# RMSNorm and SiLU on one core: one normalizing row in four moves from VectorE to GpSimd

## The chip, the cores and the metric

The kernel runs on one core of a Trainium2 chip. The metric is the device time of one execution in microseconds (us), as the median of several runs. The engines that matter here are VectorE (DVE in the profile), ScalarE (ACT), GpSimd (POOL) and SyncE (SP, which only issues loads and waits for stores). TensorE is not used.

## The reference

The input is x, 16 x 1024 rows of 512 float32 numbers, with a gamma of 512 numbers and a small eps. Each row is divided by its root mean square, multiplied by gamma, and put through SiLU:

```python
def reference(x, gamma, eps):
    rms = np.sqrt(np.mean(x ** 2, axis=-1, keepdims=True) + eps)
    x_norm = x / rms * gamma
    return (x_norm * (1.0 / (1.0 + np.exp(-x_norm)))).astype(np.float32)
```

33.55 MB are read and as many written. Gamma is drawn as ones, but the kernel multiplies by it all the same.

## The kernel before

The 16,384 rows lie 128 to a partition. One buffer in SBUF, `xb`, holds 96 rows for each partition and is used as a ring: a row is loaded into it, normalized in place, put through SiLU in place, and stored from it. Loads are transfers of 4 rows for each partition (1 MB) twice, then of 8, then seven of 16 (4 MB); stores are two of 8, six of 16 and two of 8. SyncE issues the loads in order; those of the last 32 rows wait for the stores that free their place in the ring. ScalarE issues the stores.

The unit of compute is a chunk of four rows for each partition, `cn = 4`, so that there are K = 32 units. All engines walk over the units k in order, each with its own written order, and meet at counting semaphores:

- ScalarE, `square(k)`: squares row 3 of the unit with a running sum into `ms` (L169), and rows 0 to 2 into a PSUM buffer `sq`, one of two (L176). In its order the steps are square(k), a store that is due, `swish(k - 2)`.
- VectorE, `sums(k)`: one reduction of the three squared rows from PSUM into `ms` (L218). Its order is sums(k), then `norm(k - 1)`.
- GpSimd: for each k it adds eps to four sums, `aeps` (L151, which waits for the reduction by `s_sum`), and raises them to the power -1/2, `rstd` (L158, which waits for L151 by `s_eps`). It announces the result by `s_rstd`.
- VectorE, `norm(k)`: four instructions, one for each row, each a multiply by the row's rstd and by gamma in one pass over 128x512 elements (L229). The first waits for `s_rstd`, the last announces `s_norm`.
- ScalarE, `swish(k)`: one SiLU over the four rows (L188), which waits for `s_norm` and announces `s_swish` to the stores.

Gamma comes in by a small transfer issued from ScalarE into `gamma4`, which GpSimd clears first (L146); VectorE spreads it over the partitions into `gamma_sb` (L242) between the first two reductions and announces `s_gamma`.

Of the kernel before, what the change touches and what calls it, by code (L numbers as in the profile page):

```python
# [9 lines left out]
def kernel(  # L10
# [7 lines left out]
    nc = tc.nc  # L18
    P = nc.NUM_PARTITIONS
    AF = mybir.ActivationFunctionType  # L20
    ALU = mybir.AluOpType
# [3 lines left out]
    xf = x.flatten_outer_dims()  # L25
    of = out.flatten_outer_dims()
    R, D = xf.shape

    groups = [8, 8] + [16] * 7
    G = len(groups)
    assert sum(groups) * P == R, R
    begin = [sum(groups[:g]) for g in range(G)]
    ring = 96
    loads = [(0, 0, 4), (0, 4, 4), (1, 0, 8)] + [(g, 0, 16) for g in range(2, G)]
    stores = [(0, 0, 8), (1, 0, 8)] + [(g, 0, 16) for g in range(2, G - 1)]
    stores += [(G - 1, 0, 8), (G - 1, 8, 8)]
    early = 2
    cn = 4  # L40
    n_sq = 3


    chunks = []
    new = list(range(len(loads)))
    for g in range(G):
        for c in range(0, groups[g], cn):
            need_now = [
                i for i in new if loads[i][0] == g and loads[i][1] < c + cn
            ]  # L50
            new = [i for i in new if i not in need_now]
            chunks.append(((begin[g] + c) % ring, need_now))
    assert not new
    K = len(chunks)

    ends = [-(-(begin[g] + r + n) // cn) for g, r, n in stores]

    inv_d = 1.0 / float(D)
    eps_f = float(eps)
# [6 lines left out]
    def sbuf(name, shape, dt=fp32):  # L66
        return nc.alloc_sbuf_tensor(name, shape, dt).ap()

    xb = sbuf("xb", [P, ring, D])
    gamma4 = sbuf("gamma4", [P, D])  # L70
    gamma_sb = sbuf("gamma_sb", [P, D])
# [4 lines left out]
    rstd = sbuf("rstd", [P, K, cn])  # L76
    sq = [nc.alloc_psum_tensor(f"sq{i}", [P, 4, D], fp32).ap() for i in range(2)]

    ld = [nc.alloc_semaphore(f"ld{t}") for t in range(len(loads))]
    st = [nc.alloc_semaphore(f"st{t}") for t in range(len(stores))]  # L80
    scratch = nc.dram_tensor("scratch", [P, 16], fp32, kind="Internal").ap()
    blank = sbuf("blank", [P, 16])
    s_blank = nc.alloc_semaphore("s_blank")
# [4 lines left out]
    s_gamma = nc.alloc_semaphore("s_gamma")  # L88
# [3 lines left out]
    s_eps = nc.alloc_semaphore("s_eps")  # L92
    s_rstd = nc.alloc_semaphore("s_rstd")
    s_norm = nc.alloc_semaphore("s_norm")
    s_swish = nc.alloc_semaphore("s_swish")

    def need(ins, sem, value):
        return ins.wait_op(sem, value, "sem-ge")

    def dram(ap, piece):  # L100
        g, r, n = piece
        rows = ap[begin[g] * P : (begin[g] + groups[g]) * P]
        return rows.rearrange("(p n) d -> p n d", n=groups[g])[:, r : r + n, :]

    def buf(piece):
        g, r, n = piece
        at = (begin[g] + r) % ring
        assert at + n <= ring
        return xb[:, at : at + n, :]


    stored_by_sync = set()

    def load(i):
        g, r, n = loads[i]
        old = begin[g] + r - ring
        for u, (h, q, m) in enumerate(stores):
            if (
                begin[h] + q < old + n and old < begin[h] + q + m
                and u not in stored_by_sync  # L120
            ):
                nc.sync.wait_ge(st[u], 16)
                stored_by_sync.add(u)
        return nc.sync.dma_start(
            out=buf(loads[i]), in_=dram(xf, loads[i])
        ).then_inc(ld[i], 16)

    entry = nc.main_func.blocks[0].instructions
    here = nc.cur_bb.bb.instructions
    for t in range(early):  # L130
        ins = load(t).ins
        assert here[-1] is ins or here[-1].name == ins.name
        here.pop()
        at = next(
            i for i, other in enumerate(entry)
            if other.engine == mybir.EngineType.SP
            and isinstance(other, mybir.InstDrain)
        )
        entry.insert(at, ins)
    for t in range(early, len(loads)):  # L140
        load(t)
    nc.sync.wait_ge(s_scratch, 16)

# [5 lines left out]
    for k in range(K):  # L149
        need(  # L150
            nc.gpsimd.tensor_scalar(  # L151
                out=aeps[:, k, :], in0=ms[:, k, :], scalar1=eps_f, scalar2=None,
                op0=ALU.add,
            ),
            s_sum, k + 1,
        ).then_inc(s_eps, 1)
        need(
            nc.gpsimd.tensor_tensor(  # L158
                out=rstd[:, k, :], in0=aeps[:, k, :], in1=neg_half, op=ALU.pow
            ),  # L160
            s_eps, k + 1,
        ).then_inc(s_rstd, 1)


    def square(k):
        at, landing = chunks[k]
        for i in landing:
            nc.scalar.wait_ge(ld[i], 16)  # L168
        acc = nc.scalar.activation(  # L169
            out=junk[k % 2], in_=xb[:, at + n_sq, :], func=AF.Square,  # L170
            scale=inv_d**0.5, accum_out=ms[:, k, n_sq : n_sq + 1],
        )
        if k >= 2:
            need(acc, s_acc, k - 1)
        acc.then_inc(s_acc, 1)
        square = nc.scalar.activation(  # L176
            out=sq[k % 2][:, 0:n_sq, :], in_=xb[:, at : at + n_sq, :],
            func=AF.Square, scale=inv_d**0.5,
        )
        if k >= 2:  # L180
            need(square, s_sum, k - 1)
        square.then_inc(s_sq, 1)

    def swish(k):
        at, _ = chunks[k]
        rows = xb[:, at : at + cn, :]
        need(
            nc.scalar.activation(out=rows, in_=rows, func=AF.Silu), s_norm, k + 1  # L188
        ).then_inc(s_swish, 1)

    def store(t):
        need(
            nc.scalar.dma_start(out=dram(of, stores[t]), in_=buf(stores[t])),
            s_swish, ends[t],
        ).then_inc(st[t], 16)

    need(nc.scalar.dma_start(out=scratch, in_=blank), s_blank, 1).then_inc(
# [7 lines left out]
    stored = 0  # L205
    for k in range(K + 3):
        if k < K:
            square(k)
        while stored < len(stores) and ends[stored] <= k - 2:
            store(stored)  # L210
            stored += 1
        if 2 <= k < K + 2:
            swish(k - 2)
# [9 lines left out]
        ).then_inc(s_sum, 1)  # L223

    def norm(k):
        at, _ = chunks[k]
        for j in range(cn):
            row = xb[:, at + j, :]
            ins = nc.vector.scalar_tensor_tensor(  # L229
                out=row, in0=row, scalar=rstd[:, k, j : j + 1], in1=gamma_sb,  # L230
                op0=ALU.mult, op1=ALU.mult,
            )
            if j == 0:
                need(ins, s_rstd, k + 1)
        ins.then_inc(s_norm, 1)

    for k in range(K + 1):
        if k < K:
            sums(k)
        if k == 0:  # L240
            need(
                nc.vector.stream_shuffle(gamma_sb, gamma4, [0] * 32), s_gld, 16  # L242
            ).then_inc(s_gamma, 1)
        if k == 1:
            nc.vector.wait_ge(s_gamma, 1)
        if k >= 1:
            norm(k - 1)


    for t in range(len(stores)):  # L250
        if t not in stored_by_sync:
            nc.sync.wait_ge(st[t], 16)

# [34 lines left out]
```

## Time and profile before

| what | us |
|---|---|
| three runs | 160.24, 160.31, 160.80 (median 160.31) |
| the profiled execution, whole | 160.24 |
| its span in the profile | 158.9 |
| VectorE busy | 138.9 (87%) |
| ScalarE busy | 125.4 (79%) |
| GpSimd busy | 90.1 (57%) |

The span runs from the first to the last instruction of the profile; the rest of the profiled execution's time lies around it. A line of a group of instructions reads: source line, engine, operation, output and inputs with their shapes, count; then busy us in all, mean ns of one; then the idle time of the engine just before them, and what ended most of it. In a timeline a line is start us, duration us, engine, source line, operation, and in brackets the idle time before it. Neighbouring instructions of one line are merged there (x4). In a table of windows, each engine's busy us in a stretch is followed by the count of its instructions; the last three numbers are TensorE's granted clock (not used here), the busy share of the DMA engines, and GB/s moved.

### The profile page before, as it was taken

How to read it: one execution, taken by the hardware profiler on the slowest of the kernel's cores; microseconds unless marked ns; L12 is line 12 of the kernel's file. 1: busy time of each engine (PE TensorE's matmuls, PEld its weight loads, DVE VectorE, ACT ScalarE, POOL GpSimd, SP SyncE). 2: the span in 40 equal slices, each digit the busy share in tenths (PEclk: the TensorE clock that was granted, in tenths of full speed). 3: DMA queues.
4: the chain of work that ended last, by engine and by line, in shares of the span. 5: the costliest groups of instructions: out<-in, count | busy, mean ns of one | idle time of the engine just before them, and what ended most of it. 6: DMA issues, size and time to landing. Idle time of an engine off the chain costs nothing.

```text
span 158.9 us, 436 instructions
## 1 busy us (share of the span) xinstructions
DVE 138.9 (87%) x162; ACT 125.4 (79%) x129; POOL 90.1 (57%) x71
## 2 busy tenths in 40 slices
DVE  0149999999999999999999999999999999999300
ACT  0845988888888889988888888888998898883600
POOL 2035444444455555588888899888888874445000
DMA  7999999999999999999999999999999999999896
GB/s 239 439 481 429 396 462 392 400 433 421 429 447 404 433 429 489 404 404 478 429 398 421 487 412 412 478 421 404 412 495 412 412 454 437 412 412 495 359 450 280
DMA packets 3035, 67.15 MB, mean 423 GB/s; under 512 B 468, under 2 KB 468, under 8 KB 472
## 3 DMA queue, kind: packets, MB, share of 16 engines
q1 hardware_dynamic: 1440, 33.56, 49.9%
q10 hardware_dynamic: 1592, 33.57, 49.1%
q14 instruction: 3, 0.02, 0.0%
HBM read 33.56 MB, written 33.56 MB: 422 GB/s over the span
## 4 chain that ended last, share of the span: by engine, by line
DMA 54%; DVE 34%; ACT 4%; issue 1%; POOL 0%; ACTq 0%; POOLq 0%
DMA xb<-in_x_dram 31%; DVE xb L229 22%; DMA out_dram<-xb 18%; DVE ms L218 12%; DMA gamma<-in_gamma_dram 5%; ACT xb L188 2%; ACT sq L176 1%; ACT junk L169 0%; DVE gamma_sb L242 0%; POOL gamma L146 0%; POOL blank L145 0%; ACTq L168 0%; POOLq L64 0%
## 5 line engine op out<-in xcount | busy, mean ns | idle before, releaser
L229 DVE SCALAR_TENSOR_TENSOR xb<-xb,rstd,gamma_sb 128x512 f32<-128x512 f32 x128 | 88.1, 770 | 0.0
L151 POOL TENSOR_SCALAR aeps<-ms 128x4 f32<-128x4 f32 x32 | 50.5, 1577 | 50.9 <-DVE ms L218 50.9
L188 ACT ACTIVATE xb<-xb 128x2048 f32<-128x2048 f32 x32 | 61.2, 1911 | 17.4 <-DVE xb L229 17.4
L218 DVE TENSOR_REDUCE ms<-sq 128x3 f32<-128x1536 f32 x32 | 56.8, 1774 | 7.3 <-ACT sq L176 7.2
L176 ACT ACTIVATE sq<-xb 128x1536 f32<-128x1536 f32 x32 | 45.9, 1434 | 0.0
L158 POOL TENSOR_TENSOR rstd<-aeps,neg_half 128x4 f32<-128x4 f32 x32 | 38.8, 1212 | 2.7
L169 ACT ACTIVATE junk<-xb 128x512 bf16<-128x512 f32 x32 | 19.8, 618 | 3.9 <-DMA xb<-in_x_dram 3.9
L169 ACT ACTIVATION_READ_ACCUMULATOR junk<-xb 128x1 f32 x32 | 6.0, 188 | 0.0
L204 ACT ACT_TABLE_LOAD x1 | 1.3, 1283 | 3.6 <-issue 3.6
L242 DVE LOAD_MASK_SELECT gamma_sb<-gamma x1 | 0.0, 14 | 2.2 <-DMA gamma<-in_gamma_dram 2.2
L145 POOL MEMSET blank<- 128x16 f32 x1 | 0.1, 112 | 1.5 <-POOLq L64 1.5
L242 DVE STREAM_SHUFFLE gamma_sb<-gamma 128x512 f32<-128x512 f32 x1 | 0.7, 716 | 0.0
L146 POOL MEMSET gamma<- 128x512 f32 x1 | 0.5, 526 | 0.0
L269 POOL MEMSET const-float32-0.0<- 128x1 f32 x1 | 0.1, 99 | 0.2 <-issue 0.2
L269 POOL MEMSET const-uint8-127<- 128x1 uint8 x1 | 0.1, 103 | 0.0
L269 POOL MEMSET const-bfloat16-1.0<- 128x1 bf16 x1 | 0.1, 102 | 0.0
L147 POOL MEMSET neg_half<- 128x4 f32 x1 | 0.1, 102 | 0.0
L269 POOL MEMSET const-float32-1.0<- 128x1 f32 x1 | 0.1, 99 | 0.0
## 6 DMA issues: line engine op xcount, KB each, us to landing
xb<-in_x_dram SPq DMA_DIRECT2D x7, 4096.0 KB, 49.5
out_dram<-xb ACTq DMA_DIRECT2D x6, 4096.0 KB, 29.0
out_dram<-xb ACTq DMA_DIRECT2D x4, 2048.0 KB, 15.0
xb<-in_x_dram SPq DMA_DIRECT2D x2, 1024.0 KB, 6.1
xb<-in_x_dram SPq DMA_DIRECT2D x1, 2048.0 KB, 10.7
scratch<-blank ACTq DMA_DIRECT2D x1, 8.0 KB, 8.0
gamma<-in_gamma_dram ACTq DMA_DIRECT2D x1, 8.0 KB
```

Of the source, the lines that this page charges most:

```text
L145: nc.gpsimd.memset(blank, 0.0).then_inc(s_blank, 1)
L146: nc.gpsimd.memset(gamma4, 0.0).then_inc(s_zero, 1)
L151: nc.gpsimd.tensor_scalar(out=aeps[:, k, :], in0=ms[:, k, :], scalar1=eps_f, scalar2=None, op0=ALU.add,),
L158: nc.gpsimd.tensor_tensor(out=rstd[:, k, :], in0=aeps[:, k, :], in1=neg_half, op=ALU.pow),
L169: acc = nc.scalar.activation(out=junk[k % 2], in_=xb[:, at + n_sq, :], func=AF.Square, scale=inv_d**0.5, accum_out=ms[:, k, n_sq : n_sq + 1],)
L176: square = nc.scalar.activation(out=sq[k % 2][:, 0:n_sq, :], in_=xb[:, at : at + n_sq, :], func=AF.Square, scale=inv_d**0.5,)
L188: nc.scalar.activation(out=rows, in_=rows, func=AF.Silu), s_norm, k + 1
L204: nc.scalar.preload_act_table_set("silu_and_others")
L218: nc.vector.tensor_reduce(out=ms[:, k, 0:n_sq], in_=sq[k % 2][:, 0:n_sq, :], op=ALU.add, axis=mybir.AxisListType.X,),
L229: ins = nc.vector.scalar_tensor_tensor(out=row, in0=row, scalar=rstd[:, k, j : j + 1], in1=gamma_sb, op0=ALU.mult, op1=ALU.mult,)
L242: nc.vector.stream_shuffle(gamma_sb, gamma4, [0] * 32), s_gld, 16
L269: nc = _bacc.Bacc("TRN2", target_bir_lowering=False, num_devices=1)
```

## The change

VectorE's `norm` covers three rows of a unit (`n_vec = 3`). GpSimd normalizes the fourth with two instructions after each rstd: a multiply by the row's rstd, and a multiply by `gamma_sb`, both in place over 128x512 elements; the second waits for the first by the new semaphore `s_scaled`, and announces `s_rest`. Before its first such row GpSimd waits for `s_gamma`. ScalarE's `swish(k)` waits for `s_rest` besides `s_norm`. The lists of transfers are written in another way, with one size for loads and stores alike, so that the first two stores move 4 rows each in place of one of 8, and the last load of 16 rows becomes two of 8. The lines below leave out what only renames.

```diff
-    groups = [8, 8] + [16] * 7
+    sizes = [4, 4, 8] + [16] * 6 + [8, 8]
     ring = 96
-    loads = [(0, 0, 4), (0, 4, 4), (1, 0, 8)] + [(g, 0, 16) for g in range(2, G)]
-    stores = [(0, 0, 8), (1, 0, 8)] + [(g, 0, 16) for g in range(2, G - 1)]
-    stores += [(G - 1, 0, 8), (G - 1, 8, 8)]
     early = 2
     cn = 4
     n_sq = 3
+    n_vec = 3
...
+    s_rest = nc.alloc_semaphore("s_rest")
+    s_scaled = nc.alloc_semaphore("s_scaled")
...
             s_eps, k + 1,
         ).then_inc(s_rstd, 1)
+        if k == 0:
+            nc.gpsimd.wait_ge(s_gamma, 1)
+        _, at, _ = chunks[k]
+        for j in range(n_vec, cn):
+            row = xb[:, at + j, :]
+            done = k * (cn - n_vec) + j - n_vec
+            need(
+                nc.gpsimd.tensor_scalar(
+                    out=row, in0=row, scalar1=rstd[:, k, j : j + 1], scalar2=None,
+                    op0=ALU.mult,
+                ),
+                s_rstd, k + 1,
+            ).then_inc(s_scaled, 1)
+            ins = need(
+                nc.gpsimd.tensor_tensor(out=row, in0=row, in1=gamma_sb, op=ALU.mult),
+                s_scaled, done + 1,
+            )
+        ins.then_inc(s_rest, 1)
...
     def swish(k):
-        at, _ = chunks[k]
+        _, at, _ = chunks[k]
         rows = xb[:, at : at + cn, :]
+        nc.scalar.wait_ge(s_rest, k + 1)
         need(
             nc.scalar.activation(out=rows, in_=rows, func=AF.Silu), s_norm, k + 1
         ).then_inc(s_swish, 1)
...
     def norm(k):
-        at, _ = chunks[k]
-        for j in range(cn):
+        _, at, _ = chunks[k]
+        for j in range(n_vec):
             row = xb[:, at + j, :]
             ins = nc.vector.scalar_tensor_tensor(
                 out=row, in0=row, scalar=rstd[:, k, j : j + 1], in1=gamma_sb,
```

More of the change, by code (lines that the diff above doesn't have):

```diff
@@ L27 @@
     R, D = xf.shape
-    groups = [8, 8] + [16] * 7
-    G = len(groups)
-    assert sum(groups) * P == R, R
-    begin = [sum(groups[:g]) for g in range(G)]
+    sizes = [4, 4, 8] + [16] * 6 + [8, 8]
     ring = 96
-    loads = [(0, 0, 4), (0, 4, 4), (1, 0, 8)] + [(g, 0, 16) for g in range(2, G)]
-    stores = [(0, 0, 8), (1, 0, 8)] + [(g, 0, 16) for g in range(2, G - 1)]
-    stores += [(G - 1, 0, 8), (G - 1, 8, 8)]
     early = 2
@@ L41 @@
     n_sq = 3
[L44 to L53, printed above, removed]
-    K = len(chunks)
-    ends = [-(-(begin[g] + r + n) // cn) for g, r, n in stores]
+    n_vec = 3
+    N = sum(sizes)
+    assert N * P == R, (N, R)
+    tiles = []
+    done = 0
+    for sz in sizes:
+        assert done % ring + sz <= ring
+        tiles.append((done * P, sz, done % ring))
+        done += sz
+    T = len(tiles)
+    chunks = [
+        (t, r, r == at)
+        for t, (_, sz, at) in enumerate(tiles)
+        for r in range(at, at + sz, cn)
+    ]
+    K = len(chunks)
+    ends = []
+    e = 0
+    for sz in sizes:
+        e += sz // cn
+        ends.append(e)
     inv_d = 1.0 / float(D)
@@ L77 @@
     sq = [nc.alloc_psum_tensor(f"sq{i}", [P, 4, D], fp32).ap() for i in range(2)]
-    ld = [nc.alloc_semaphore(f"ld{t}") for t in range(len(loads))]
-    st = [nc.alloc_semaphore(f"st{t}") for t in range(len(stores))]
+    ld = [nc.alloc_semaphore(f"ld{t}") for t in range(T)]
+    st = [nc.alloc_semaphore(f"st{t}") for t in range(T)]
     scratch = nc.dram_tensor("scratch", [P, 16], fp32, kind="Internal").ap()
@@ L98, in need, with dram, buf, load @@
         return ins.wait_op(sem, value, "sem-ge")
[L100 to L109, printed above, removed]
-    stored_by_sync = set()
[L114 to L126, printed above, removed]
+    def dram(ap, t):
+        first, sz, _ = tiles[t]
+        return ap[first : first + P * sz].rearrange("(p n) d -> p n d", n=sz)
+    def buf(t):
+        _, sz, at = tiles[t]
+        return xb[:, at : at + sz, :]
+    stored_by_sync = set()
+    def load(t):
+        _, sz, at = tiles[t]
+        waits = [
+            u for u in range(t)
+            if tiles[u][2] < at + sz and at < tiles[u][2] + tiles[u][1]
+            and u not in stored_by_sync
+        ]
+        for u in waits:
+            nc.sync.wait_ge(st[u], 16)
+            stored_by_sync.add(u)
+        return nc.sync.dma_start(out=buf(t), in_=dram(xf, t)).then_inc(ld[t], 16)
     entry = nc.main_func.blocks[0].instructions
@@ L139 @@
         entry.insert(at, ins)
-    for t in range(early, len(loads)):
+    for t in range(early, T):
         load(t)
@@ L162 @@
         ).then_inc(s_rstd, 1)
+        if k == 0:
[16 more added lines that the diff above has]
+        ins.then_inc(s_rest, 1)
     def square(k):
-        at, landing = chunks[k]
-        for i in landing:
-            nc.scalar.wait_ge(ld[i], 16)
+        t, at, first = chunks[k]
+        if first:
+            nc.scalar.wait_ge(ld[t], 16)
         acc = nc.scalar.activation(
@@ L192, in store @@
         need(
-            nc.scalar.dma_start(out=dram(of, stores[t]), in_=buf(stores[t])),
-            s_swish, ends[t],
+            nc.scalar.dma_start(out=dram(of, t), in_=buf(t)), s_swish, ends[t]
         ).then_inc(st[t], 16)
@@ L208 @@
             square(k)
-        while stored < len(stores) and ends[stored] <= k - 2:
+        while stored < T and ends[stored] <= k - 2:
             store(stored)
@@ L247 @@
             norm(k - 1)
-    for t in range(len(stores)):
+    for t in range(T):
         if t not in stored_by_sync:
```

## The prediction, made before the changed kernel was run

> **What bounds the kernel now.** I read the page first: engine totals, DMA, chain, groups.
>
> ```profile
> span 158.9 us, 436 instructions
> DVE 138.9 (87%) x162; ACT 125.4 (79%) x129; POOL 90.1 (57%) x71
> DMA packets 3035, 67.15 MB, mean 423 GB/s; under 512 B 468, under 2 KB 468, under 8 KB 472
> DMA 54%; DVE 34%; ACT 4%; issue 1%; POOL 0%; ACTq 0%; POOLq 0%
> ...
> L229 DVE SCALAR_TENSOR_TENSOR xb<-xb,rstd,gamma_sb 128x512 f32<-128x512 f32 x128 | 88.1, 770 | 0.0
> L151 POOL TENSOR_SCALAR aeps<-ms 128x4 f32<-128x4 f32 x32 | 50.5, 1577 | 50.9 <-DVE ms L218 50.9
> ```
>
> VectorE looks like the one to relieve, but the chain is mostly DMA. The windows by stage say why:
>
> ```profile
> 11.00:46.00 35.00, 34.82 (x42) 29.14 (x31) 16.37 (x16) 1.00 1.01 429
> 46.00:126.00 80.00, 80.00 (x93) 71.44 (x73) 59.95 (x37) 1.00 1.00 431
> 126.00:150.00 24.00, 22.36 (x28) 19.02 (x18) 11.67 (x10) 1.00 1.00 433
> 150.00:159.00 9.00, 0.00 (x0) 0.37 (x1) 0.00 (x0) 1.00 0.84 360
> ```
>
> The last two numbers of a row are the DMA's busy share and GB/s: from 11 to 150 us the transfers are full at about 431 GB/s. VectorE is full too, so two limits lie on top of each other, and relieving VectorE alone frees nothing that the transfers can use.
>
> The odd row is L151: adding eps to 128x4 numbers averages 1,577 ns. GpSimd's timeline shows it:
>
> ```profile
> 1.95 0.53 POOL L146 MEMSET gamma<- 128x512 f32 x1
> 2.41 0.10 POOL L147 MEMSET neg_half<- 128x4 f32 x1
> 9.09 0.23 POOL L151 TENSOR_SCALAR aeps<-ms 128x4 f32<-128x4 f32 x1 [6.57 <-DVE ms L218]
> 9.40 1.04 POOL L158 TENSOR_TENSOR rstd<-aeps,neg_half 128x4 f32<-128x4 f32 x1
> 13.62 0.66 POOL L151 TENSOR_SCALAR aeps<-ms 128x4 f32<-128x4 f32 x1 [3.18 <-DVE ms L218]
> 14.36 1.39 POOL L158 TENSOR_TENSOR rstd<-aeps,neg_half 128x4 f32<-128x4 f32 x1
> ...
> 65.40 2.65 POOL L151 TENSOR_SCALAR aeps<-ms 128x4 f32<-128x4 f32 x1 [2.19 <-DVE ms L218]
> 68.13 1.04 POOL L158 TENSOR_TENSOR rstd<-aeps,neg_half 128x4 f32<-128x4 f32 x1
> ```
>
> and VectorE's beside it:
>
> ```profile
> 65.20 2.76 DVE L229 SCALAR_TENSOR_TENSOR xb<-xb,rstd,gamma_sb 128x512 f32<-128x512 f32 x4
> 67.85 1.78 DVE L218 TENSOR_REDUCE ms<-sq 128x3 f32<-128x1536 f32 x1
> ```
>
> At 9.09 VectorE is idle: 0.23 us. At 13.62 the four multiplies have just begun and the same add takes 0.66, ending as the first of them ends. At 65.40 it takes 2.65, ending when all four have ended. So a GpSimd instruction that reads SBUF gets nowhere while VectorE's two-input multiply runs; it slips in between two of them (16 of 32 units) or is locked out until all are over (15). The reduction, which reads PSUM, does not hold it: the power at 68.13 keeps its 1.04 beside it. Today all this is free, because VectorE asks for rstd one reduction later than it is ready.
>
> **The change, part by part.** *Off VectorE:* one multiply of four per unit. Their pitch is 0.66 us (67.85-65.20 over 4), the reduction's is 1.66; a unit goes from 4.32 to 3.65 us, 21 us over 32 units. Alone this is worth nothing, with the DMA at share 1.00 to 150 us.
>
> *Onto GpSimd:* a 128x512 multiply by rstd and a 128x512 multiply by gamma per unit. No such row exists. The memsets give the cost of 512 columns in one pass: 0.53-0.10 = 0.43 us. One input: 0.23 (the free add) + 0.43 = 0.66; bounds 0.53 (the memset itself) and 1.09 (read and write passes in turn). Two inputs: 0.23 + 2x0.43 = 1.09, the operands read in turn; bounds 0.66 (all passes together) and 1.52 (three in turn). I take 0.66 and 1.09, the middles, since the memset shows one pass and nothing shows a second stream.
>
> [...]
>
> *What queues behind them.* GpSimd runs in order: the add and power for unit k+1 now stand behind both multiplies of unit k, and VectorE's multiplies of k+1 wait for that power. GpSimd alone needs 0.66 + 1.09 + 0.23 + 1.04 = 3.02, with four waits of 0.08 (9.40 less the add's end at 9.32) 3.34 us per unit. That would fit. But VectorE's three multiplies are released by the same semaphore, s_rstd, as GpSimd's first, and the two exclude each other. Locked out: 0.08 + 1.99 (three pitches) + 0.11 (770 less 660 ns, the last one's end) + 0.66 + 0.08 + 1.09 + 0.08 + 0.23 + 0.08 + 1.04 = 5.44 us. Slipping in by turns, VectorE first: 0.08 + 0.66 + 0.66 + 0.66 + 1.09 + 0.66 + 0.23 + 0.08 + 1.04 = 5.16. By turns, GpSimd first, the third VectorE multiply falls beside the power: 0.08 + 0.66 + 0.66 + 1.09 + 0.66 + 0.66 + 1.04 = 4.85. The trace has slips and lockouts about evenly, so I take (5.44 + 5.00)/2 = 5.22 us per unit. Whether VectorE is held by a running GpSimd pass in turn isn't shown; if it isn't, GpSimd is held instead, and the sum stands.
>
> [...]
>
> *ScalarE* gets a second wait before each silu (for s_rest). Behind it stand the squares of the unit three later, two 5.22 us cycles before they are needed; silu, square and reduction take 1.91 + 2.25 + 1.76 = 5.9 of these 10.4, so it costs nothing. *Stores and loads:* the first store splits into two of 4 rows, the last load into two of 8; one more issue each (0.34 us on ScalarE's queue, which waits 17.4 us in all today), same bytes: nothing.
>
> **The sum**, on the profiled execution (160.24 us, span 158.9, so 1.3 around it; the median shown is 160.31):
> - Unit 0's passes start when gamma lands (11.9) and end at 13.9; VectorE's first three multiplies then run, and rstd of unit 1 is ready at 16.2 (slip) to 17.3 (lockout): 16.8.
> - 30 units at 5.22: 156.6, to 173.4.
> - The last unit's multiplies on both engines: 0.08 + 2.10 + 0.66 + 0.08 + 1.09 = 4.0, to 177.4.
> - Last silu 1.91 and its wait: 2.0, to 179.4.
> - Last store. Before, issue at 150.40 to the end took 8.5; 3.24 MB (360 GB/s in 9 us) moved after 150.0, 2.10 of them its own, 0.17 before the issue, so 0.97 MB, 2.2 us, belonged to the store ahead. At the slower pace that one is done: 6.3, to 185.7.
> - Around the span 1.3: **187.0 us**. In short 30.4 + 30c, c the cycle.
>
> **The rivals.** *The passes interleave* (not slower). If a 512-column pass of GpSimd isn't stopped by the multiplies, only a 4-column one waiting at its first read, then c is 3.34 for GpSimd and 3.65 for VectorE, both under the transfers; the time stays 160.2, a few tenths either way, for the DMA had share 1.00. It decides from c = 4.3 down (30.4 + 30x4.3 = 159.4). For it: VectorE itself never stretched when GpSimd slipped in (pitch 0.66 in both). Against: 2.65 for a four-column add; and at the bounds of cost below, by turns, c is only just 4.29. Chance 0.10, of which 0.03 faster.
>
> *Dear passes.* At 1.09 and 1.52 with lockout c is 6.30, and the last unit grows by 0.86: 220 us. For it: GpSimd's power takes 1.04 for four columns, so its arithmetic can be slow. Chance 0.11.
>
> *Always by turns* is the forecast's own low side: 30.4 + 30x5.0 = 180.4; always locked out 193.6.
>
> **How the numbers follow.** The forecast's case, exclusion at middling prices, holds 0.79. About half of the spread of the bounds either way of 5.22 gives c of 4.65 to 5.8: 169.9 to 204.4, so 170 to 205. What is left out is the two rivals, 0.21. Half a percent (0.8 us) is about what a measurement can tell here; faster 0.03, same 0.07, slower 0.90.
>
> **What would show it.** Right: VectorE gains an idle group before its first multiply, released by GpSimd's power, of 1 to 2 us per unit; GpSimd's idle before the eps add falls from 50.9 us to nearly none and its busy share passes 90%; the chain runs over GpSimd's lines; the DMA share falls to about 0.85. The step on the multiplies is right if each takes longer than 0.66 and 1.09 only where VectorE's multiplies lie beside it. Wrong: VectorE's wait stays at zero, or passes of 512 columns keep one duration whether VectorE multiplies or not (interleaving), or take over 1.1 and 1.5 with VectorE idle (dear).

## The result and the profile after

The changed kernel takes 177.63 us (four runs, 177.50 to 177.64), against 160.34 us for the kernel before (four runs, the three shown before among them): a ratio of 1.107, 95% interval 1.1048 to 1.1092. It is 17.3 us slower. The forecast was 187.0 us in a range of 170 to 205, with a chance of 0.90 for slower. The profiled execution took 177.64 us, its span 176.3. (Of two kernels below, seven of ten executions without the gamma pass and one of two with half-width passes took 5 to 8 us longer than the fastest of the same kernel, for a cause that isn't known; these enter no comparison of times.)

The page of the changed kernel, its totals, its chain and the groups of the steps at issue:

```profile
span 176.3 us, 504 instructions
DVE 155.5 (88%) x130; ACT 125.2 (71%) x129; POOL 149.0 (85%) x135
POOL 84%; DMA 5%; issue 4%; ACT 1%; DVE 0%; POOLq 0%; ACTq 0%
...
L246 DVE SCALAR_TENSOR_TENSOR xb<-xb,rstd,gamma_sb 128x512 f32<-128x512 f32 x96 | 103.8, 1133 | 1.2 <-POOL rstd L157 1.2
...
L169 POOL TENSOR_SCALAR xb<-xb,rstd 128x512 f32<-128x512 f32 x32 | 51.0, 1594 | 4.9 <-DVE gamma_sb L259 1.8
L176 POOL TENSOR_TENSOR xb<-xb,gamma_sb 128x512 f32<-128x512 f32 x32 | 43.7, 1365 | 2.7
...
L150 POOL TENSOR_SCALAR aeps<-ms 128x4 f32<-128x4 f32 x32 | 20.7, 648 | 6.4 <-DVE ms L235 6.4
```

The chain now runs over GpSimd for 84% of the span, and its 50.9 us of idle time before the eps add are down to 6.4. The first surprise is VectorE: it has a quarter fewer multiplies, yet is busy for longer, 155.5 against 138.9 us. Each multiply takes 1,133 ns in the mean where it took 770. Its wait for GpSimd is inside its instructions, and shows in no idle column.

The windows of the changed kernel, in the columns explained before:

```profile
11.00:46.00 35.00, 34.84 (x31) 25.68 (x28) 32.20 (x28) 1.00 1.01 427
46.00:126.00 80.00, 80.00 (x67) 63.86 (x68) 75.65 (x66) 1.00 1.01 429
126.00:164.00 38.00, 36.76 (x32) 27.98 (x28) 35.88 (x33) 1.00 0.70 297
```

To 126 us the transfers are still full, loading ahead into the ring; then the share falls to 0.70, because the remaining stores wait for compute. VectorE shows 80.00 of 80 us busy and GpSimd 75.65, the rest being semaphore waits of 0.07 to 0.09 us between its instructions: both look saturated at once. The timeline of one unit says how that can be (ScalarE's lines are left out):

```profile
85.81 1.58 POOL L169 TENSOR_SCALAR xb<-xb,rstd 128x512 f32<-128x512 f32 x1
86.08 3.28 DVE L246 SCALAR_TENSOR_TENSOR xb<-xb,rstd,gamma_sb 128x512 f32<-128x512 f32 x3
...
87.47 1.35 POOL L176 TENSOR_TENSOR xb<-xb,gamma_sb 128x512 f32<-128x512 f32 x1
88.80 0.66 POOL L150 TENSOR_SCALAR aeps<-ms 128x4 f32<-128x4 f32 x1
89.29 1.75 DVE L235 TENSOR_REDUCE ms<-sq 128x3 f32<-128x1536 f32 x1
...
89.54 1.04 POOL L157 TENSOR_TENSOR rstd<-aeps,neg_half 128x4 f32<-128x4 f32 x1
```

A unit takes 4.87 us (the next first pass starts at 90.68). Shorter windows of the same timeline show the three multiplies one by one. The second runs from 86.96 to 87.70; the first and the third are:

```profile
86.08 0.95 DVE L246 SCALAR_TENSOR_TENSOR xb<-xb,rstd,gamma_sb 128x512 f32<-128x512 f32 x1
...
87.62 1.75 DVE L246 SCALAR_TENSOR_TENSOR xb<-xb,rstd,gamma_sb 128x512 f32<-128x512 f32 x1
```

The third multiply starts 0.15 us after GpSimd's gamma pass and ends 0.55 us after that pass ends (88.82), where the shortest of the 96 multiplies takes 0.735: it stood until the pass was over, or nearly so. Then GpSimd's eps add, which takes 0.23 at 8.88 with VectorE idle, stands in turn until that multiply ends, and takes 0.66. The rstd pass is another matter: it runs 1.58 us, and VectorE's first multiply starts and ends inside it, only some 0.2 us longer than the usual 0.735. So in this order the rstd pass holds VectorE at most near its start, and the gamma pass holds it nearly throughout.

### The profile page after: what moved, and what is told of

The parts are those of the page before. It is cut to its first block, busy times and chain, and to the rows that moved or that the text cites. A ratio compares the mean times of both kernels' runs of the same rounds, so it can differ in the third digit from the quotient of the medians.

```text
span 176.3 us, 504 instructions
## 1 busy us (share of the span) xinstructions
DVE 155.5 (88%) x130; ACT 125.2 (71%) x129; POOL 149.0 (85%) x135
## 3 DMA queue, kind: packets, MB, share of 16 engines
q10 hardware_dynamic: 1736, 33.57, 44.8%
q1 hardware_dynamic: 1584, 33.56, 44.8%
## 4 chain that ended last, share of the span: by engine, by line
POOL 84%; DMA 5%; issue 4%; ACT 1%; DVE 0%; POOLq 0%; ACTq 0%
POOL xb L169 29%; POOL xb L176 25%; POOL rstd L157 19%; POOL aeps L150 11%; DMA gamma<-in_gamma_dram 5%; ACT xb L206 1%; DVE gamma_sb L259 0%; POOL gamma L145 0%; POOL blank L144 0%; ACTq L204 0%; POOLq L163 0%; POOLq L66 0%
## 5 line engine op out<-in xcount | busy, mean ns | idle before, releaser
L246 DVE SCALAR_TENSOR_TENSOR xb<-xb,rstd,gamma_sb 128x512 f32<-128x512 f32 x96 | 103.8, 1133 | 1.2 <-POOL rstd L157 1.2
L235 DVE TENSOR_REDUCE ms<-sq 128x3 f32<-128x1536 f32 x32 | 55.8, 1745 | 7.0 <-ACT sq L193 7.0
L169 POOL TENSOR_SCALAR xb<-xb,rstd 128x512 f32<-128x512 f32 x32 | 51.0, 1594 | 4.9 <-DVE gamma_sb L259 1.8
L176 POOL TENSOR_TENSOR xb<-xb,gamma_sb 128x512 f32<-128x512 f32 x32 | 43.7, 1365 | 2.7
L157 POOL TENSOR_TENSOR rstd<-aeps,neg_half 128x4 f32<-128x4 f32 x32 | 33.5, 1048 | 2.7
L150 POOL TENSOR_SCALAR aeps<-ms 128x4 f32<-128x4 f32 x32 | 20.7, 648 | 6.4 <-DVE ms L235 6.4
```

The source lines that it names most:

```text
L150: nc.gpsimd.tensor_scalar(out=aeps[:, k, :], in0=ms[:, k, :], scalar1=eps_f, scalar2=None, op0=ALU.add,),
L157: nc.gpsimd.tensor_tensor(out=rstd[:, k, :], in0=aeps[:, k, :], in1=neg_half, op=ALU.pow),
L169: nc.gpsimd.tensor_scalar(out=row, in0=row, scalar1=rstd[:, k, j : j + 1], scalar2=None, op0=ALU.mult,),
L176: nc.gpsimd.tensor_tensor(out=row, in0=row, in1=gamma_sb, op=ALU.mult),
L235: nc.vector.tensor_reduce(out=ms[:, k, 0:n_sq], in_=sq[k % 2][:, 0:n_sq, :], op=ALU.add, axis=mybir.AxisListType.X,),
L246: ins = nc.vector.scalar_tensor_tensor(out=row, in0=row, scalar=rstd[:, k, j : j + 1], in1=gamma_sb, op0=ALU.mult, op1=ALU.mult,)
```

## The experiments

**The lists alone.** VectorE takes all four rows again, and GpSimd no passes; the new lists of transfers stay. The edit takes out the passes and the wait of `swish` for `s_rest` as well.

```diff
-    n_vec = 3
+    n_vec = 4
...
```

> Only the new lists of loads and stores, with VectorE normalizing all four rows and GpSimd none. If the lists cost nothing (prediction): 160.3 us, within 0.3 either way, VectorE's unit at 4.32 us. Rival, the two small early stores or the split last load disturb the transfers: 161 us or more with a DMA share under 1.00 between 11 and 150 us.

Measured: 160.09 us, ratio 0.9976 (0.9965 to 0.9988). The lists cost nothing; they are even a quarter of a percent ahead of the kernel before. Where the 0.4 us come from isn't settled. So the whole loss, 17.5 us against this kernel, belongs to the moved row.

**VectorE out of the way.** Its multiplies shrink to 16 columns.

```diff
-                out=row, in0=row, scalar=rstd[:, k, j : j + 1], in1=gamma_sb,
-                op0=ALU.mult, op1=ALU.mult,
+                out=row[:, 0:16], in0=row[:, 0:16], scalar=rstd[:, k, j : j + 1],
+                in1=gamma_sb[:, 0:16], op0=ALU.mult, op1=ALU.mult,
```

> VectorE's three multiplies cover 16 of 512 columns (the other 496 of rows 0 to 2 stay unnormalized), so that VectorE hardly reads SBUF; GpSimd's work is whole. Theory A, GpSimd's own work fills its cycle: its passes stay at 1.58 and 1.35 us, only the eps add falls from 0.66 to 0.23, the cycle goes from 4.87 to about 4.44 and the time to 177.6 - 30 x 0.43 = 165 us. Theory B, exclusion as in the prediction: the passes fall to about 0.66 and 1.09, the cycle to 3.3, and the transfers bound the time at 160 us.

Measured: 162.70 us, ratio 1.0133 (1.0112 to 1.0153). Two lines of the timeline and the group of the add:

```profile
87.05 1.69 POOL L169 TENSOR_SCALAR xb<-xb,rstd 128x512 f32<-128x512 f32 x1
88.82 1.26 POOL L176 TENSOR_TENSOR xb<-xb,gamma_sb 128x512 f32<-128x512 f32 x1
```
```profile
L150 POOL TENSOR_SCALAR aeps<-ms 128x4 f32<-128x4 f32 x32 | 7.4, 231 | 6.4 <-DVE ms L235 6.4
```

The passes are dear by themselves: 1.69 and 1.26 us with only the narrow multiplies beside the first (1.58 in the first two units), far from the 0.66 and 1.09 of the forecast. But the cycle is 4.45 us (from 82.60 to 87.05), so with these prices alone GpSimd would lose 2 us, not 17. Theory A's cycle was right; its time, 165, was 2.3 us high, mostly since the start and the last unit also lose their collisions (rstd of unit 1 is ready at 16.2 instead of 17.4, and from the last rstd to the last silu it takes 3.2 instead of 3.7).

**No gamma pass.**

```diff
...
-            ins = need(
-                nc.gpsimd.tensor_tensor(out=row, in0=row, in1=gamma_sb, op=ALU.mult),
-                s_scaled, done + 1,
             )
```

> GpSimd's second pass, the multiply by gamma, is left out for the fourth row (gamma is drawn as ones). Theory A: GpSimd's cycle is 1.58 + 0.23 to 0.66 + 1.04 + 0.25 = 3.1 to 3.5 us, below VectorE's and below the transfers; 160.3 us, with the first pass still at 1.58 us. Theory B: the first pass at 0.66, else the same time. Rival C, that any reading pass of GpSimd between two powers delays VectorE: over 165 us.

Measured: 160.12 us in the profiled execution, ratio 1.0022 (0.9974 to 1.0071). The rstd pass stays at 1.58 to 1.60 us, the units follow each other every 3.8 to 3.9 us and VectorE's three multiplies take 2.07 us again. GpSimd's add and power still stand beside the multiplies (0.66 and 1.38 us), but with one pass instead of two its cycle has room for that; theory C falls.

**The power ahead of the passes.** GpSimd computes rstd of unit k+1 before the passes of unit k.

```diff
...
+    for k in range(K + 1):
+        if k < K:
+            stats(k)
...
+        if k >= 1:
+            fourth(k - 1)
```

> GpSimd's order is changed: the eps add and power of unit k+1 come before the two passes of unit k, so that VectorE's rstd never stands behind a pass. Theory A (a sum of GpSimd's own work): the same instructions, so a cycle of 4.5 to 4.9 us and 167 to 178 us. Theory C, the loss is the place of the power behind the passes: VectorE runs at its own pace and the time returns to 160 to 162 us.

Measured: 196.01 us, ratio 1.2216 (1.2183 to 1.2249). Neither theory had this. The waits of this kernel, longest first:

```profile
DVE ms L243 <- ACT sq L201: 57.4, 30, 7.0
ACT xb L214 <- POOL xb L176: 55.6, 32, 4.8
POOL aeps L150 <- DVE ms L243: 22.0, 17, 6.4
```

They form a ring: the reduction waits for the squares, the squares stand behind a silu on ScalarE, the silu waits for GpSimd's gamma pass, and GpSimd waits for the reduction. Moving the passes one unit later shortened this ring from three units to two, and two units now take 10.9 us (eps adds at 84.33 and 95.21). The forecast had priced this ring at nothing; in the order of the change that was right, by one unit.

**The same, with ScalarE one unit further behind.** Shown is what comes on top of the edit before.

```diff
...
-    for k in range(K + 3):
+    for k in range(K + 4):
...
-        while stored < T and ends[stored] <= k - 2:
+        while stored < T and ends[stored] <= k - 3:
...
-        if 2 <= k < K + 2:
-            swish(k - 2)
+        if 3 <= k < K + 3:
+            swish(k - 3)
```

> As the kernel with the power ahead of the passes, but ScalarE's silu and stores walk one unit further behind its squares (three units instead of two). Theory D, that the 196 us came from the loop passes - silu - squares - reduction - eps add, which spanned two units: the loop now spans three, and the cycle falls back to GpSimd's own sum, 4.45 to 4.9 us, 165 to 178 us. Theory E, that the order itself makes GpSimd and VectorE collide more: it stays over 185 us.

Measured: 176.17 us, ratio 1.0974 (1.0956 to 1.0993), with a cycle of 4.77 us. Theory D holds, and with the ring out of the way the order of power and passes moves the time by only 1.5 us of the 17. So the wait for a power queued behind the passes isn't what costs.

**No eps add.**

```diff
-            nc.gpsimd.tensor_scalar(
-                out=aeps[:, k, :], in0=ms[:, k, :], scalar1=eps_f, scalar2=None,
-                op0=ALU.add,
+            nc.gpsimd.tensor_tensor(
+                out=rstd[:, k, :], in0=ms[:, k, :], in1=neg_half, op=ALU.pow
             ),
             s_sum, k + 1,
-        ).then_inc(s_eps, 1)
...
```

> The changed kernel without the eps add: the power reads the mean square itself (eps is left out). Theory S, the add's 0.66 and its wait of 0.08 simply leave the sum: the cycle is 4.87 - 0.74 = 4.13 us, under the transfers, 160 us. Theory H, a hand-over by turns: VectorE's third multiply stands until GpSimd's gamma pass ends, and GpSimd's next read, whichever it is, stands until that multiply ends; the power then stretches in place of the add, the cycle is about 1.58 + 0.08 + 1.35 + 0.55 + 1.04 + 0.09 = 4.7 us and the time 172 us.

Measured: 170.47 us, ratio 1.0620 (1.0604 to 1.0636). The cycle is 4.66 us, and in its timeline the power stretches to 1.48 us in place of the add:

```profile
88.00 3.07 DVE L239 SCALAR_TENSOR_TENSOR xb<-xb,rstd,gamma_sb 128x512 f32<-128x512 f32 x3
88.39 1.46 POOL L169 TENSOR_TENSOR xb<-xb,gamma_sb 128x512 f32<-128x512 f32 x1
89.82 1.48 POOL L150 TENSOR_TENSOR rstd<-ms,neg_half 128x4 f32<-128x4 f32 x1
```

Theory H holds, 1.5 us below its 172: what follows the gamma pass on GpSimd stretches in both kernels, the add by 0.43 us in the changed one (0.66 for 0.23), the power by 0.44 here (1.48 for 1.04). Taking 0.74 us out of GpSimd's sum gave back only 0.21 per unit.

**Half the width.** Both passes cover 256 columns.

```diff
-                    out=row, in0=row, scalar1=rstd[:, k, j : j + 1], scalar2=None,
+                    out=row[:, 0:256], in0=row[:, 0:256], scalar1=rstd[:, k, j : j + 1], scalar2=None,
...
-                nc.gpsimd.tensor_tensor(out=row, in0=row, in1=gamma_sb, op=ALU.mult),
+                nc.gpsimd.tensor_tensor(
+                    out=row[:, 0:256], in0=row[:, 0:256], in1=gamma_sb[:, 0:256],
+                    op=ALU.mult,
+                ),
```

> GpSimd's two passes cover 256 of the fourth row's 512 columns (the other half stays unnormalized). If a pass costs a fixed part and a part by column, the multiply by rstd takes 0.23 + 0.68 = 0.9 us and that by gamma 0.23 + 0.51 = 0.75; the cycle falls under 4.3 us and the time to 160 us. If the first pass is mostly a fixed cost, it stays near 1.5 us, with a cycle near 4.2.

Its times, 162.69 and 167.35 us, settle nothing about the forecast of 160. The durations, from the profile of the 167.35 us execution, do: 0.94 and 0.73 us, as expected. From 256 to 512 columns the rstd pass grows by 0.64 us and the gamma pass by 0.53: 2.5 and 2.1 ns for a column, with fixed parts of 0.3 and 0.2 us (two points each, so a straight line is assumed). The units follow each other every 3.95 us from 82 to 93 us.

**Every second unit.** GpSimd takes the fourth row of the even units only; the counts that the semaphores wait for change with it.

```diff
-        for j in range(n_vec, cn):
+        for j in range(n_vec, cn) if k % 2 == 0 else []:
...
-        for j in range(n_vec):
+        for j in range(n_vec if k % 2 == 0 else cn):
```

> GpSimd normalizes the fourth row of every second unit only; VectorE takes all four rows of the others. If the loss is GpSimd's cycle over the transfers' pace of 4.3 us, the mean of the two cycles (4.87 and about 4.3, VectorE's) lies near it and the time is 160 to 163 us. If every collision costs for itself, half of the 17 us is lost: 169 us.

Measured: 164.27 us, ratio 1.0238 (1.0223 to 1.0254), between the two forecasts of 160 to 163 and 169, so neither holds. VectorE has no gap from 46 to 126 us; a unit in which it multiplies all four rows takes 4.31 us, one in which GpSimd takes the fourth 4.67 (from 84.98 to 89.65). VectorE gives away 0.66 us of work and loses 1.0 us by collision.

**Gamma in PSUM for VectorE.** This removes the collision and leaves all the work: VectorE reads gamma from a copy in the free fourth row of one of the two buffers `sq` in PSUM, so of the two 512-column inputs of its multiply one is left in SBUF.

```diff
...
+    gamma_ps = sq[0][:, 3, :]
...
-                out=row, in0=row, scalar=rstd[:, k, j : j + 1], in1=gamma_sb,
+                out=row, in0=row, scalar=rstd[:, k, j : j + 1], in1=gamma_ps,
...
-            nc.vector.wait_ge(s_gamma, 1)
+            need(
+                nc.vector.tensor_copy(out=gamma_ps, in_=gamma_sb), s_gamma, 1
+            ).then_inc(s_gps, 1)
+            nc.vector.wait_ge(s_gps, 1)
```

> The changed kernel, but VectorE reads gamma from a copy in PSUM (an unused bank beside the squares), so that its multiplies have one SBUF input instead of two; GpSimd's work is the same. Theory H, the two engines collide over the second SBUF input: GpSimd's cycle falls to its own 4.45 us, its eps add to 0.23, VectorE's three multiplies to 2.0 to 2.2 us with an idle wait before them, and the time to about 163 us, as with narrow VectorE multiplies. Rival: any SBUF work of VectorE, its writes too, holds GpSimd: no change, 177 us.

Measured: 160.40 us, ratio 1.0001 (0.9988 to 1.0014). The whole loss is gone. A unit of its timeline:

```profile
84.20 0.23 POOL L152 TENSOR_SCALAR aeps<-ms 128x4 f32<-128x4 f32 x1
84.51 1.04 POOL L159 TENSOR_TENSOR rstd<-aeps,neg_half 128x4 f32<-128x4 f32 x1
85.58 2.06 DVE L248 SCALAR_TENSOR_TENSOR xb<-xb,rstd,sq 128x512 f32<-128x512 f32 x3
85.65 1.57 POOL L171 TENSOR_SCALAR xb<-xb,rstd 128x512 f32<-128x512 f32 x1
87.31 1.27 POOL L178 TENSOR_TENSOR xb<-xb,gamma_sb 128x512 f32<-128x512 f32 x1
```

Every instruction has its undisturbed time, though VectorE's three multiplies lie beside GpSimd's passes, but for 0.07 us. The rival, that any work of VectorE on SBUF holds GpSimd, falls: the add keeps its 0.23 and the passes 1.57 and 1.27. The cycle is 4.34 us, GpSimd's own sum, and the transfers are full from 11 to 150 us once more (share 0.99 to 1.02). My 163 was too high because I had put the cycle at 4.45.

**Gamma in PSUM, and a two-tensor rstd pass.** Shown is what comes on top of the edit before.

```diff
-                nc.gpsimd.tensor_scalar(
-                    out=row, in0=row, scalar1=rstd[:, k, j : j + 1], scalar2=None,
-                    op0=ALU.mult,
-                ),
+                nc.gpsimd.tensor_tensor(
+                    out=row, in0=row, in1=rstd[:, k, j : j + 1].to_broadcast([P, D]),
+                    op=ALU.mult,
+                ),
```

> As the kernel with gamma in PSUM, and GpSimd's first pass is a multiply of two tensors with rstd repeated along the columns, in place of a multiply by a scalar. If the pass then costs what the gamma pass does, 1.26 us, the cycle is 1.26 + 1.26 + 0.23 + 1.04 + 0.33 = 4.12 us, under the 4.3 at which the transfers take over: 160 to 161 us. If a repeated operand costs as much as the scalar form, 1.6 us: 163 us.

Measured: 160.24 us, ratio 0.9996 (0.9983 to 1.0008). The pass falls to 1.04 us and the units come every 3.8 to 3.9 us, yet the time is that of the kernel before: here the transfers decide (share 0.99 to 1.02 from 11 to 150 us).

**The two-tensor pass alone,** with gamma in SBUF for both engines; the edit is the last one without the copy.

> The changed kernel with gamma in SBUF for both engines, and only GpSimd's first pass as a multiply of two tensors. If GpSimd's own price decides: the cycle falls by 0.32 to 4.55 us, 168 us. Theory H: a two-tensor pass holds VectorE for its whole length, where the scalar form held it only at its start, so the saving is lost again in a second hand-over: cycle 4.9 to 5.1 us, 177 to 184 us.

Measured: 167.58 us, ratio 1.0448 (1.0432 to 1.0463), with a cycle of 4.57 us. Here theory H in the form I gave it was wrong: VectorE's multiplies meet only the second pass (86.06 to 87.32, the first multiply from 86.22, 1.65 us long), since its reduction (84.56 to 86.30) still runs beside the first (84.94 to 85.98). The other expectation, 4.55 us and 168 us, came out in its numbers, but not for its reason, that GpSimd's own price decides: the same instructions come every 3.8 to 3.9 us with gamma in PSUM, and here the add takes 0.67 instead of 0.23 and the power 1.39 instead of 1.04. A collision has to be laid out along the time axis; a count of colliding instructions isn't enough.

## Why the prediction was right, and where it wasn't

**The bound of the kernel before.** Right. Relieving VectorE without a collision leaves 160.4 and 160.24 us; the transfers were the limit to 150 us, and the kernels with cycles of 3.9 and 4.34 us can't be told apart in time. The point from which GpSimd decides, 4.3 us, held too: 4.34 gives 160.40, 4.45 gives 162.70, 4.49 gives 164.27, 4.57 gives 167.58, 4.66 gives 170.47 and 4.87 gives 177.63. From 4.34 to 4.87 that is 17.2 us for 0.53, or about 32 for each us of the cycle: near one for each unit. The kernel with the power first and ScalarE further behind, 4.77 and 176.17, lies some 2 us above this line; there two units' passes are left behind the last power, so that the last silu starts 6.4 us after it, against 3.7.

**The sum.** By the terms of the forecast against the profiled execution: rstd of unit 1 ready at 17.4 (forecast 16.8); 30 cycles of 4.87, 146.2 (156.6); the last unit 3.7 (4.0); the silu 2.0 (2.0); the last store 7.0 (6.3); around the span 1.3 (1.3). Together 177.6; the 9.4 us between the two lie in the cycle, 10.4, less 1.0 in the small terms.

**The cycle was nearly right by luck: two errors stood against each other.** The forecast of 5.22 was 3.34 of GpSimd's own work and 1.88 of exclusion. Measured, with the collision taken away, GpSimd's own work is 4.34 (1.57 + 1.27 + 0.23 + 1.04 and the waits), and exclusion adds 0.53. The first step that failed is the price of the passes: 0.66 and 1.09, taken from the memsets, against 1.57 and 1.27. The memsets differ by 0.43 us for 512 columns, 0.84 ns a column; between 256 and 512 columns the two passes grew by 2.5 and 2.1. The bounds on the first pass, 0.53 to 1.09, didn't even hold it. The second is the exclusion: I let two to three of VectorE's multiplies stand in GpSimd's path in each unit. In fact the first two of VectorE's multiplies lie beside the rstd pass for most of their time, which costs them 0.2 us (0.95 and 0.74 us against 0.735), and the loop that closes has one multiply: rstd pass 1.58, wait 0.08, gamma pass 1.35, the rest of the held multiply 0.55 with the add behind it 0.09, wait 0.08, power 1.04, wait 0.09, which makes 4.86. The forecast also took 1.04 for a power beside VectorE's multiplies, where its own line at 14.36 shows 1.39. Either error alone would have missed, by an estimate from these figures: the forecast's 3.34 with the measured 0.53 is 3.87, under 4.3 and so no loss at all; the measured 4.34 with the forecast's 1.88 is 6.22, some 217 us by the forecast's 30.4 + 30c.

**The signs.** The chain over GpSimd and the idle time before the add came as forecast; the share of the DMA queues over the span is 0.90 (44.8% each), not 0.85. The idle group on VectorE did not come: I had named a zero there as a sign of being wrong, but the wait sits inside the multiplies (770 to 1,133 ns). The busy share of GpSimd is 85% over the span, though 95% from 46 to 126 us. The sign on the multiplies failed too: the passes take more than 0.66 and 1.09 with nothing held as well (1.57 and 1.27 with gamma in PSUM). The dear-passes rival gave as its sign passes over 1.1 and 1.5 us with VectorE idle; the first came, the second didn't, and the sum of both, 2.84, was nearer to its 2.61 than to the forecast's 1.75. Its 220 us came from the lockout that it added. Dear passes alone cost nothing, as gamma in PSUM shows (160.40 us), but they are part of the cause: they bring GpSimd's own cycle to 4.34, the point from which it decides, so that the collision counts in full. With one pass left out the add and the power still stood (0.66 and 1.38), and the profiled execution took 160.12. The interleaving rival was half true: the rstd pass keeps its 1.58 beside VectorE's multiplies, while the gamma pass takes 1.35 against 1.27.

**Which of the two stands.** With gamma in PSUM, so with one SBUF input of VectorE's multiply instead of two, neither engine stood (160.40 us, the add at 0.23, three multiplies in 2.06). With both inputs in SBUF the gamma pass, once running, held a multiply for nearly its whole length (the multiply took 1.75 us); the rstd pass did not: a multiply of 0.95 us that starts 0.27 us into it runs to its end within its 1.58. When the multiply starts first, the rstd pass does stand. In the last unit, with no reduction ahead of it, VectorE's first multiply runs from 163.68 to 164.43, and the pass that starts 0.07 us after it takes 2.13 in place of 1.58:

```profile
163.75 2.13 POOL L169 TENSOR_SCALAR xb<-xb,rstd 128x512 f32<-128x512 f32 x1
```

**Left open.** Why the rstd pass, with one tensor, is dearer than a multiply of two (1.57 against 1.04 us in the same place, gamma in PSUM in both); why that pass holds VectorE no longer than near its start; and why the eps add sometimes slipped between multiplies and sometimes not.

## What to carry to other kernels

Before moving work between VectorE and GpSimd, ask whether VectorE will read two tensors from SBUF while GpSimd reads any: here that made a unit of 4.87 us out of 4.34. And look at the shortest GpSimd instruction: a 0.23 us add that takes 2.65 is the collision showing for free. If the work must be shared, take VectorE's second operand out of SBUF; one copy of gamma to PSUM was worth all of the 17.3 us, and left the kernel as fast as it was before the change, because the transfers decide there (share 0.99 to 1.02 to 150 us). And price an operation by a row that reads, computes and writes, not by a memset: 512 columns took 0.53 us to set, and 1.57 and 1.27 to multiply.

## What the runs showed of the hardware

VectorE's 128x512 multiply took the same with its second input in PSUM as in SBUF (2.06 us for three with gamma in PSUM, 2.07 in the kernel without the gamma pass). With gamma in PSUM, GpSimd's multiply by a scalar for each partition took 1.57 us for 128x512, its multiply by a full tensor 1.27, and that by the same scalars repeated along the columns 1.04: the scalar form, with one full tensor to read, took longer than the form with two.
